# Last feed-forward of a streaming encoder: down-projection by seven products, stream states scaled on ACT

## The chip, the cores and the metric

The kernel runs on one core of a Trainium2 chip. A core has five engines that run side by side, each with its own queue worked off in order: PE (TensorE, matrix products), DVE (VectorE, elementwise), ACT (ScalarE, elementwise and functions), POOL (GpSimd) and SP (SyncE, which here only issues transfers). PE reads its operands from the on-chip memory SBUF and accumulates in PSUM, which has eight banks of 128x512 float32. Transfers between the chip's memory and SBUF are done by 16 DMA engines. The metric is the device time of one execution in microseconds (us).

## The reference, cut to what matters

Two layers of an encoder are applied to 640 tokens of 1024 channels: 512 tokens of a new stream and 16 new tokens for each of eight running streams. Each of the six sub-layers adds its output to its input and normalises. Four of them are feed-forwards; the last sub-layer is one of these. Beside it the kernel finishes the states of the eight running streams of the sub-layer before (a Mamba-2 mixer).

```
x = layer_norm(ALPHA * x + 0.5 * swiglu(x, w_gate, w_up, w_down), g, b)      # four times
def swiglu(x, w_gate, w_up, w_down):
    return (silu(x @ w_gate) * (x @ w_up)) @ w_down          # 1024 -> 2816 -> 1024
h_new = h * exp(cs[:, -1])[..., None, None] + einsum('bsgr,bsgn,bsgrp->bgrpn', to_end, b_c, x_c)
```

Everything is float32.

## The kernel before, in words

**Phases.** `ffn0`, `mix0`, `ffn1`, `ffn2`, `mix1`, `ffn3` run one after the other, all through `ffn()` for the four feed-forwards. The width of 2816 is cut into 22 rows `f` of 128 channels.

**Float32 from three products.** Every operand is split by `split` (lines 94 and 95): ACT rounds it to a high part (a cast), DVE subtracts to get the low part. A product is then three matmuls: high by high, low by high, high by low (`mm3`, line 133).

**Gate and up.** The rows are taken in pairs by `pair`. For each pair, `operands` (lines 320 to 348) loads two blocks of weights and forms the operands of a seven-product (Strassen-Winograd) scheme, and `matrix` (line 358) does seven products of 12 matmuls of 320 columns each (line 355) in three PSUM banks of the pool `a`. Where a bank's running sum is needed twice, `keep` (line 366) copies it to SBUF by ACT into a tile `mx`; PE's next product into that bank waits for the copy. `mx` has three buffers.

**Down-projection.** After each second pair the four rows of the group before are projected by `down`. There are two forms:

- The plain form: for each of five token tiles `t` and two halves `j` of the 1024 channels, `tm_proj` does 12 matmuls of 512 columns in a bank of pool `b`, and DVE adds the bank to the residual `yacc` (line 208).
- `down7`, which the phases listed in `SEVEN` use for four of the six groups: the first four token tiles go by seven products in six banks (`x` and `w` from pool `b`, which has four, `z` from pool `a`), each product on two token tiles `tp` with six matmuls of 512 columns (line 487); the fifth tile goes the plain way (line 507). Sums of rows of the left operand are made earlier by `row_sums` (lines 440 to 445), those of the weights at lines 461 to 464. After each product, `add` takes the bank into `yacc`: for `tp` 1 by DVE (line 495), for `tp` 0 ACT scales it into a tile `ev` (line 498), which a POOL transfer adds to `yacc` (line 499). `ev` has three buffers and is held until the transfer has landed.

Before the change `SEVEN` holds `ffn1` and `ffn2`. The group of two rows at the start and the last group of four, which ends in the layer norm, are plain in every phase.

**Side work of the last phase.** `ssd_states` is a generator that `ffn` steps through at marked points, called ticks: after each gate and each up matrix, and in a plain `down` after token tiles 0, 2 and 4. A step does one of 32 states: a matmul of 48 rows (line 1145), a scaling of the loaded state `h0` by DVE (line 1148), an addition of the matmul's bank by DVE (line 1149), the store (line 1150), and the load of the next state (line 1141). `h0` has two buffers. The first phase has side work of its own (`s5_tables`); `ffn1` and `ffn2` have none.

**Order.** The program is traced as written; a scheduler at build time then orders each engine's queue by readiness in its own model of time and by program order. `tc.issue_after(x)` puts the instructions of the block that run on the engine of `x` behind `x`. A tile's buffer is given out again when all that read it are done.

Of the kernel before, what the change touches and what calls it, by code (L numbers as in the profile page):

```python
# [9 lines left out]
F32 = mybir.dt.float32  # L10
# [3 lines left out]
ALU = mybir.AluOpType  # L14
# [12 lines left out]
HALVES = ((0, 256), (256, 384))  # L27
RAWS = 4
PAIRS = 6
SEVEN = ("ffn1", "ffn2")  # L30
PHASES = ("ffn0", "mix0", "ffn1", "ffn2", "mix1", "ffn3")
LN_OF = {"ffn0": 0, "mix0": 1, "ffn1": 2, "ffn2": 3, "mix1": 4, "ffn3": 5}

# [2 lines left out]
def kernel(ctx: ExitStack, tc: tile.TileContext, I, O, phases=PHASES):  # L36
    nc = tc.nc

    def pool(name, bufs=1, stack=ctx, **kw):
        return stack.enter_context(tc.tile_pool(name=name, bufs=bufs, **kw))  # L40
# [24 lines left out]
    def bank_a():  # L65
        return bank("a")

    def bank_b():
        return bank("b")
# [141 lines left out]
    def ffn(i, ph, last, side=None):  # L211
# [3 lines left out]
        Q = T // 2  # L215
        with ExitStack() as st:
            wk = pool(f"ffn{i}_wk", 1, st, reuse_waits="tile")
            steps = side(wk) if side is not None else iter(())

            def tick(where):  # L220
# [56 lines left out]
            for r in range(2):  # L277
                w = load_w(I["w_gate"][i, 2 + r])
                first[r] = g_row()
                for c in range(2):  # L280
                    p = bank_a()[:, :Q]
# [15 lines left out]

            t2, t3 = (wk.tile([128, 4, Q], F32, name="h", bufs=4) for _ in range(2))
            for k in range(4):
                t1 = wk.tile([128, Q], F32, name="mx", bufs=3)  # L300
                minus(t3[:, k], (1, 1), (0, 1))
                minus(t1, (0, 1), (0, 0))
                for part in (hf32, lf32):
                    V.tensor_tensor(t2[:, k], t3[:, k] if part is hf32 else t2[:, k], quad(part, 0, 0)[:, k], op=ALU.add)
                split(tq[2][:, 0, k], tq[2][:, 1, k], t2[:, k])
                split(tq[1][:, 0, k], tq[1][:, 1, k], t1)
# [52 lines left out]
            def matrix(A, take):  # L359

                x, w, z = (bank_a()[:, :Q] for _ in range(3))
                e = {}

                def keep(n, ps):
                    e[n] = wk.tile([128, Q], F32, name="mx", bufs=3)
                    nc.scalar.copy(e[n], ps)  # L366


                product(x, A, 1, True)
                keep(1, x)  # L370
                product(z, A, 2, True)
                take(0, 0, z, e[1])
                product(x, A, 6, False)
                keep(2, x)
                product(w, A, 5, True)
                keep(5, w)
                product(x, A, 7, False)
                take(1, 1, x, e[5])
                product(w, A, 3, False)
                take(0, 1, w, e[2])  # L380
                product(x, A, 4, False)
                take(1, 0, x, None)

            def pair(f, before=None):
# [26 lines left out]
                for n, take in (("w_gate", gate), ("w_up", up)):  # L411
# [10 lines left out]
                    matrix(A, take)  # L422
                    if n == "w_up" and ph in SEVEN and f < NF - 4:
                        row_sums(f)
# [8 lines left out]
            def row_sums(f):  # L433


                v = [wk.tile([128, 512], F32, name="ev", bufs=3) for _ in range(2)]
                s1, s2, s3, s4 = (v[n // 2][:, n % 2 * 256:n % 2 * 256 + 256].rearrange("p (n c) -> p n c", n=2)
                                  for n in range(4))
                p, q = by_pairs(hf[f]), by_pairs(hf[f + 1])
                V.tensor_tensor(s1, p[:, :, 1], q[:, :, 1], op=ALU.add)  # L440
                V.tensor_tensor(s2, s1, p[:, :, 0], op=ALU.subtract)
                V.tensor_tensor(s3, p[:, :, 0], p[:, :, 1], op=ALU.subtract)
                V.tensor_tensor(s4, q[:, :, 0], s2, op=ALU.subtract)
                o = hs[f] = wk.tile([128, 2, 1024], F32R, name="hs", bufs=2)
                for n in range(2):
                    split(o[:, 0, 512 * n:512 * n + 512], o[:, 1, 512 * n:512 * n + 512], v[n])

            def down7(fs):


                raws, direct = {}, {}
                for f in fs:
                    raws[f] = raw_tile()
                    nc.sync.dma_start(raws[f], I["w_down"][i, f])
                for f in fs:
                    direct[f] = two_units()
                    split2(direct[f], raws[f])

                for f in fs[::2]:
                    (b11, b12), (b21, b22) = ((r[:, :512], r[:, 512:]) for r in (raws[f], raws[f + 1]))  # L460
                    V.tensor_tensor(b22, b22, b12, op=ALU.subtract)
                    V.tensor_tensor(b12, b12, b11, op=ALU.subtract)
                    V.tensor_tensor(b11, b22, b11, op=ALU.add)
                    V.tensor_tensor(b21, b21, b11, op=ALU.subtract)
                T = {}
                for r in range(2):
                    for f in fs[::2]:
                        T[f + r] = two_units()
                        split2(T[f + r], raws[f + r])

                def left(f, p, tp):
                    tok = lambda k, a: ht[f + k][:, :, 256 * tp + 128 * a:256 * tp + 128 * a + 128]
                    if p in (1, 2, 4):
                        return tok(*{1: (0, 0), 2: (1, 0), 4: (1, 1)}[p])
                    o = 256 * {5: 0, 6: 1, 7: 2, 3: 3}[p] + 128 * tp
                    return hs[f][:, :, o:o + 128]

                def right(f, p):
                    return {1: direct[f][:, 0], 2: direct[f + 1][:, 0], 3: direct[f + 1][:, 1],
                            6: T[f][:, 0], 5: T[f][:, 1], 4: T[f + 1][:, 0], 7: T[f + 1][:, 1]}[p]  # L480

                def product(ps, tp, p, first):
                    n = 0
                    for f in fs[::2]:
                        a, b = left(f, p, tp), right(f, p)
                        for u, v in ((0, 0), (1, 0), (0, 1)):
                            nc.tensor.matmul(ps, a[:, u], b[:, v], start=(first and n == 0), stop=(n == 5),
                                             skip_group_check=True)
                            n += 1

                def add(ps, t, j):

                    if t // 2:
                        ya = yacc[:, t, j * 512:j * 512 + 512]
                        V.scalar_tensor_tensor(ya, ps, 0.5 / ALPHA, ya, op0=ALU.mult, op1=ALU.add)
                        return
                    e = wk.tile([128, 512], F32, name="ev", bufs=3)
                    nc.scalar.mul(e, ps, 0.5 / ALPHA)  # L498
                    nc.gpsimd.dma_start(yacc[:, t, 512 * j:512 * j + 512], e, accum_op=ALU.add)  # L499

                t = NT - 1
                for j in range(2):
                    pb = bank_a()
                    mm3(pb, [(ht[f][:, 0, t * 128:t * 128 + 128], ht[f][:, 1, t * 128:t * 128 + 128]) for f in fs],
                        [(direct[f][:, j, 0], direct[f][:, j, 1]) for f in fs])
                    ya = yacc[:, t, j * 512:j * 512 + 512]
                    state["acc"] = V.scalar_tensor_tensor(ya, pb, 0.5 / ALPHA, ya, op0=ALU.mult, op1=ALU.add).ins
                x, w = ([bank_b() for _ in range(2)] for _ in range(2))
                z = [bank_a() for _ in range(2)]
                for p, ps, a, j in ((1, x, 0, 0), (2, z, 0, 0), (5, w, 1, 1), (6, x, 0, 1), (3, w, 0, 1), (7, x, 1, 1),  # L510
                                    (4, x, 1, 0)):
                    for tp in range(2):
                        product(ps[tp], tp, p, p in (1, 2, 5))
                        add(ps[tp], 2 * tp + a, j)

            def down(fs, norm=None):
                if ph in SEVEN and len(fs) == 4 and norm is None:
# [603 lines left out]
    def ssd_states(wk):  # L1121

        el8 = wk.tile([128, 4, 8, 8], F32, name="el8")
        nc.sync.dma_start(el8.rearrange("p g b h -> p g (b h)"), ssd["el"])
        for g, b2, q in ((g, b2, q) for g in range(4) for b2 in range(2) for q in range(2)):
# [11 lines left out]
                        nc.sync.dma_start(xb[rows, 512:640], src(sb, 512, 640))  # L1137
            for h in range(2):
                n = 4 * h + 2 * b2 + q
                h0 = wk.tile([128, 512], F32, name="h0", bufs=2)  # L1140
                nc.sync.dma_start(h0, I["ssd_h0"][g, n])
                yield
                rows = slice(64 * h, 64 * h + 48)
                pst = bank_b()
                nc.tensor.matmul(pst, xb[rows, 512:640].bitcast(F32R), xb[rows, 0:512].bitcast(F32R),  # L1145
                                 start=True, stop=True)
                h4 = h0.rearrange("p (h d) -> p h d", d=64)
                nc.vector.tensor_tensor(h4, h4, el8[:, g, n, :, None].to_broadcast([128, 8, 64]), op=ALU.mult)
                nc.vector.tensor_tensor(h0, h0, pst, op=ALU.add)
                nc.sync.dma_start(O["ssd_s"][g, n], h0)  # L1150

# [514 lines left out]
```

## Time and profile before

| | |
|---|---|
| median of 3 runs | 2604.51 us (2600.36 to 2605.74) |
| the profiled execution | 2604.51 us, its span 2602.8 us |
| last feed-forward's stage, first to last product of its pairs | 2205.1 to 2567 us |
| its states' matmuls | 32, first at 2193.0, last at 2541.8 us |
| groups of `down7` before | four in `ffn1`, four in `ffn2` |

The span runs from the first to the last instruction; 1.7 us of the execution lie outside it. In the rows shown below, a row of the timeline gives the start in us, the length in us from the start of the first to the end of the last instruction, the engine, the line, the tiles written and read, and how many instructions it merges; a bracket at the end tells how long the engine stood idle before it and for whom. The ends of matmuls are modelled, so their pace is read from start to start. A row of the groups gives, behind the bar, the busy us of all and the mean ns of one.

### The profile page before, as it was taken

The numbers are of one execution on the slowest core, as the hardware profiler recorded it, in microseconds if no ns is written. First come the engines' busy times: TensorE is split into PE (matmuls) and PEld (weight loads), VectorE is DVE, ScalarE is ACT, GpSimd is POOL, SyncE is SP. The second block draws the span as 40 slices with busy tenths as digits, with TensorE's granted clock in tenths as the row PEclk, the third lists the DMA queues.
The fourth block names the chain that finished last, engine by engine and source line by source line (L and its number), as shares of the span: only waits on it lengthen the run. The fifth ranks groups of instructions, "written<-read, shape, count | busy, mean of one in ns | idle before, by whom it ended". The sixth has DMA issues, their size and how long they took to land. (4 is left out here: it accounts for less than half of the span.)

```text
span 2602.8 us, 40675 instructions
## 1 busy us (share of the span) xinstructions
PE 2532.5 (97%) x15577; PEld 2294.5 (88%) x15577; DVE 2037.3 (78%) x3726; ACT 1214.9 (47%) x2332; POOL 285.8 (11%) x412
## 2 busy tenths in 40 slices
PE   9999999999969999999999999999999999999998
PEld 8999999887648999998999999889889879998887
DVE  7788777667857988887888887777676799876668
ACT  4443444346533555554455554566565443443332
POOL 0000002110011000003000001311111150000001
PEclk9999999999979999999999999999999999999999
DMA  5332334542211244443144334356564622443442
GB/s 181 106 106 84 112 111 139 168 149 89 82 61 49 76 116 118 118 110 114 49 123 113 102 108 142 112 176 192 162 199 141 236 70 96 157 140 112 133 137 93
DMA packets 173810, 317.43 MB, mean 122 GB/s; under 512 B 19968, under 2 KB 90752, under 8 KB 173104
## 3 DMA queue, kind: packets, MB, share of 16 engines
q1 hardware_dynamic: 163792, 293.83, 35.5%
q0 software_dynamic: 9824, 21.01, 3.9%
q8 instruction: 122, 2.00, 0.3%
q14 instruction: 72, 0.59, 0.1%
HBM read 259.56 MB, written 40.54 MB: 115 GB/s over the span
## 5 line engine op out<-in xcount | busy, mean ns | idle before, releaser
L95 DVE TENSOR_TENSOR w<-raw,w 128x512 fp32r<-128x512 f32 (+1 forms) x617 | 536.9, 893 | 91.9 <-ACT w L94 90.3
L94 ACT CAST w<-raw 128x512 fp32r<-128x512 f32 (+1 forms) x617 | 451.3, 771 | 303.2 <-PE bank L133 113.8
L133 PE MATMUL bank<-xhi,w 128*128 128x256 f32 (+2 forms) x2528 | 557.4, 312 | 14.2 <-ACT xhi L94 6.8
L355 PE MATMUL bank<-xhi,w 128*128 128x320 f32 x2432 | 541.9, 310 | 0.7 <-ACT mx L366 0.4
L133 PEld LDWEIGHTS bank<-xhi,w 128*128 128x128 f32 x2528 | 422.9, 189 | 26.2 <-ACT xhi L94 7.8
L133 PE MATMUL bank<-w,h 128*128 128x512 f32 x1872 | 437.0, 391 | 0.0
L355 PE MATMUL bank<-T,w 128*128 128x320 f32 x2736 | 425.9, 309 | 0.4 <-ACT mx L366 0.4
L133 PEld LDWEIGHTS bank<-w,h 128*128 128x128 f32 x1872 | 348.1, 188 | 75.4 <-issue 3.4
L355 PEld LDWEIGHTS bank<-xhi,w 128*128 128x128 f32 x2432 | 406.0, 188 | 8.3 <-issue 4.4
L355 PEld LDWEIGHTS bank<-T,w 128*128 128x128 f32 x2736 | 406.3, 188 | 1.7 <-ACT mx L366 0.6
L133 PE MATMUL bank<-xlo,w 128*128 128x256 f32 (+2 forms) x1264 | 392.4, 311 | 3.9 <-DVE xlo L95 3.8
L355 PE MATMUL bank<-xlo,w 128*128 128x320 f32 x1216 | 375.0, 308 | 0.0
L133 PEld LDWEIGHTS bank<-xlo,w 128*128 128x128 f32 x1264 | 238.9, 189 | 6.5 <-DVE xlo L95 5.1
L355 PEld LDWEIGHTS bank<-xlo,w 128*128 128x128 f32 x1216 | 228.0, 188 | 0.3
L208 DVE SCALAR_TENSOR_TENSOR yacc<-bank,yacc 128x512 f32<-128x512 f32 x160 | 109.5, 687 | 81.1 <-PE bank L133 80.2
L366 ACT COPY mx<-bank 128x320 f32<-128x320 f32 x228 | 96.5, 424 | 133.3 <-PE bank L355 132.6
L95 DVE TENSOR_TENSOR w<-sw,w 128x1024 fp32r<-128x1024 f32 x76 | 93.0, 1223 | 51.4 <-ACT w L94 51.2
L94 ACT CAST w<-sw 128x1024 fp32r<-128x1024 f32 x76 | 79.8, 1050 | 100.0 <-DVE sw L334 99.0
L499 POOL DMA_DIRECT2D yacc<-ev x56 | 48.6, 902 | 652.1 <-ACT ev L498 597.9
L133 PE MATMUL bank<-w,og 128*128 128x512 f32 x432 | 106.3, 400 | 2.8 <-DVE og L1460 2.8
L133 PEld LDWEIGHTS bank<-w,og 128*128 128x128 f32 x432 | 80.6, 191 | 21.1 <-DVE og L1460 4.6
L394 ACT ACTIVATE s<-s 128x320 f32<-128x320 f32 x108 | 50.8, 471 | 88.4 <-DVE s L392 88.2
(416 smaller groups left out, 3306.4 us busy)
## 6 DMA issues: line engine op xcount, KB each, us to landing
raw<-in_w_gate_dram SPq DMA_DIRECT2D x88, 512.0 KB, 3.8
raw<-in_w_up_dram SPq DMA_DIRECT2D x88, 512.0 KB, 4.0
raw<-in_w_down_dram SPq DMA_DIRECT2D x88, 512.0 KB, 3.6
raw<-in_m_in_dram SPq DMA_DIRECT2D x52, 512.0 KB, 4.6
yacc<-ev POOLq DMA_DIRECT2D x56, 256.0 KB, 4.2
raw<-in_m_out_dram SPq DMA_DIRECT2D x24, 512.0 KB, 3.8
csb<-cs_d SPq DMA_DIRECT2D x20, 512.0 KB, 5.1
h<-in_ssd_h_dram SPq DMA_DIRECT2D x16, 512.0 KB, 6.1
```

The lines of the kernel that those rows point to most:

```text
L94: nc.scalar.copy(hi, src)
L95: return nc.vector.tensor_tensor(lo, src, hi.bitcast(F32), op=ALU.subtract)
L133: state["pe"] = nc.tensor.matmul(ps, a, b, start=(k == 0), stop=(k == n - 1)).ins
L208: state["acc"] = nc.vector.scalar_tensor_tensor(ya, pb, scale, ya, op0=ALU.mult, op1=ALU.add).ins
L355: nc.tensor.matmul(ps, A[p][:, a, k * 128:k * 128 + 128], B[p][b][:, k, :], start=(first and n == 0), stop=(n == 11), skip_group_check=True)
L366: nc.scalar.copy(e[n], ps)
L394: state["silu"] = nc.scalar.activation(t, ps, AF.Silu).ins
L499: nc.gpsimd.dma_start(yacc[:, t, 512 * j:512 * j + 512], e, accum_op=ALU.add)
```

## The change

1. `ffn3` joins `SEVEN`: four of its six groups go through `row_sums` and `down7`. `down7` gets three ticks of its own, at its start and after the products numbered 5 and 3.
2. The scaling of a state goes from one DVE instruction of 128x512 to eight ACT instructions of 128x64, one for each head, with a scale for each partition.
3. In the phases that have side work (`ffn0` and `ffn3`), `mx` and `ev` have two buffers in place of three.
4. `h0` of the states has one buffer in place of two, and the room on chip for the descriptors of POOL's transfers is halved.

```
-SEVEN = ("ffn1", "ffn2")
+SEVEN = ("ffn1", "ffn2", "ffn3")
...
+            few = side is not None
...
-                    e[n] = wk.tile([128, Q], F32, name="mx", bufs=3)
+                    e[n] = wk.tile([128, Q], F32, name="mx", bufs=2 if few else 3)
...
-                v = [wk.tile([128, 512], F32, name="ev", bufs=3) for _ in range(2)]
+                v = [wk.tile([128, 512], F32, name="ev", bufs=2 if few else 3) for _ in range(2)]
...
-                    e = wk.tile([128, 512], F32, name="ev", bufs=3)
+                    e = wk.tile([128, 512], F32, name="ev", bufs=2 if few else 3)
...
                 t = NT - 1
+                tick(0)
                 for j in range(2):
...
                         add(ps[tp], 2 * tp + a, j)
+                    if p in (5, 3):
+                        tick(2 if p == 5 else 4)
...
-                h0 = wk.tile([128, 512], F32, name="h0", bufs=2)
+                h0 = wk.tile([128, 512], F32, name="h0", bufs=1)
...
-                h4 = h0.rearrange("p (h d) -> p h d", d=64)
-                nc.vector.tensor_tensor(h4, h4, el8[:, g, n, :, None].to_broadcast([128, 8, 64]), op=ALU.mult)
+                for k in range(8):
+                    nc.scalar.mul(h0[:, 64 * k:64 * k + 64], h0[:, 64 * k:64 * k + 64], el8[:, g, n, k:k + 1])
...
-    nc = _bacc.Bacc("TRN2", target_bir_lowering=False, num_devices=1, dynamic_dma_scratch_size=4096)
+    nc = _bacc.Bacc("TRN2", target_bir_lowering=False, num_devices=1, dynamic_dma_scratch_size=2048)
```

More of the change, by code (lines that the diff above doesn't have):

```diff
@@ L299, in ffn @@
             for k in range(4):
-                t1 = wk.tile([128, Q], F32, name="mx", bufs=3)
+                t1 = wk.tile([128, Q], F32, name="mx", bufs=2 if few else 3)
                 minus(t3[:, k], (1, 1), (0, 1))
```

## The prediction

> **What bounds the kernel now.** I read the page's head first, then the waits of the last feed-forward's stage, then the chain that ended last inside it, then two stretches side by side: one of `ffn1`, where `down7` already runs, and one of `ffn3`.
>
> ```profile
> span 2602.8 us, 40675 instructions
> PE 2532.5 (97%) x15577; PEld 2294.5 (88%) x15577; DVE 2037.3 (78%) x3726; ACT 1214.9 (47%) x2332; POOL 285.8 (11%) x412
> ...
> 2218.61 12.51 PE bank L355 x84
> 2231.11 0.43 PE bank L1145
> ...
> 850.00:1180.00 330.00, 329.84 (x2000) 310.94 (x2000) 278.34 (x407) 174.48 (x267) 24.39 (x29) 1.00 0.41 111
> 2206.00:2541.00 335.00, 335.00 (x1928) 302.31 (x1928) 244.61 (x361) 123.92 (x200) 0.00 (x0) 1.00 0.42 135
> ```
>
> The third and fourth rows are from the chain of waits between 2200 and 2260 us, which is made of PE alone: a matrix (84 matmuls, 12.51 us), a state's matmul (0.43), the next matrix. The last two rows are the stretches; the columns behind the length are PE, PEld, DVE, ACT, POOL busy, granted clock, DMA share, GB/s. PE has no gap in the second stretch, the clock is full, DVE is at 244.61/335 = 73%, ACT at 37%. A modelled busy time alone proves little; the pace does:
>
> ```profile
> 976.45 5.63 PE L133 MATMUL bank<-w,h 128*128 128x512 f32 x24
> 987.36 11.04 PE L487 MATMUL bank<-w,hs 128*128 128x512 f32 x48
> 998.24 1.52 PE L487 MATMUL bank<-w,h 128*128 128x512 f32 x6
> 1050.47 5.63 PE L133 MATMUL bank<-w,h 128*128 128x512 f32 x24
> ...
> 2257.34 5.78 PE L133 MATMUL bank<-w,h 128*128 128x512 f32 x24
> 2263.48 11.18 PE L133 MATMUL bank<-w,h 128*128 128x512 f32 x48
> 2274.59 0.50 PE L1145 MATMUL bank<-xb 48*128 48x512 f32 x1
> 2338.24 5.76 PE L133 MATMUL bank<-w,h 128*128 128x512 f32 x24
> ```
>
> From start to start, 48 matmuls of `down7` take 998.24 - 987.36 = 10.88 us, 0.2267 each. In `ffn3`, 48 of the plain form take 2274.59 - 2263.48 = 11.11, the little more being the state matmuls at both ends. A group (two pairs and a down) takes 1050.47 - 976.45 = 74.02 us in `ffn1` and 2338.24 - 2257.34 = 80.90 in `ffn3`. So PE's instruction stream is the time of this stage: fewer matmuls shorten it, and work on other engines is free until PE waits for it.
>
> **Part 1, the seven products.** A plain group is 5 token tiles x 2 halves x 12 = 120 matmuls of 512 columns. `down7` is 24 for the fifth tile and 7 x 2 x 6 = 84, so 108. Four groups save 4 x 12 = 48 matmuls x 0.2267 = **10.9 us**, and nothing else is on PE's stream. The two groups' periods agree: 80.90 - 2.72 (12 x 0.2267) - 74.02 leaves 4.16 for seven states, 0.59 each, near the 0.43 of a state's row plus refilling beside it. A group of the new `ffn3` should take 80.90 - 2.72 = 78.2 us.
>
> What it adds stands in these groups of instructions, of the whole trace:
>
> ```profile
> L208 DVE SCALAR_TENSOR_TENSOR yacc<-bank,yacc 128x512 f32<-128x512 f32 x160 | 109.5, 687 | 81.1 <-PE bank L133 80.2
> L495 DVE SCALAR_TENSOR_TENSOR yacc<-bank,yacc 128x512 f32<-128x512 f32 x56 | 38.5, 688 | 44.3 <-PE bank L487 44.3
> L498 ACT ACTIVATE ev<-bank 128x512 f32<-128x512 f32 x56 | 33.4, 597 | 76.5 <-PE bank L487 76.2
> L95 DVE TENSOR_TENSOR w<-raw,w 128x512 fp32r<-128x512 f32 x400 | 276.7, 719 | 51.1 <-ACT w L94 50.5
> L95 DVE TENSOR_TENSOR w<-raw,w 128x1024 fp32r<-128x1024 f32 x216 | 261.1, 1219 | 40.7 <-ACT w L94 39.8
> L94 ACT CAST w<-raw 128x512 fp32r<-128x512 f32 x400 | 232.2, 622 | 96.0 <-PE bank L355 32.0 <-issue 17.0 <-PE bank L133 15.0
> L94 ACT CAST w<-raw 128x1024 fp32r<-128x1024 f32 x216 | 220.3, 1049 | 207.2 <-PE bank L133 98.8 <-DVE raw L334 72.2 <-DVE yacc L208 18.1
> L461 DVE TENSOR_TENSOR raw<-raw 128x512 f32<-128x512 f32 x16 | 10.3, 682 | 0.0
> L440 DVE TENSOR_TENSOR ev<-hf 128x256 f32<-128x256 f32 x16 | 6.7, 416 | 0.0
> L94 ACT CAST hs<-ev 128x512 fp32r<-128x512 f32 x32 | 19.5, 615 | 17.3 <-DVE ev L441 17.3
> L95 DVE TENSOR_TENSOR hs<-ev,hs 128x512 fp32r<-128x512 f32 x32 | 21.8, 686 | 0.0
> L1148 DVE TENSOR_TENSOR h<-h,el 128x512 f32<-128x512 f32 x32 | 21.8, 685 | 3.8 <-DMA h<-in_ssd_h_dram 3.6
> ```
>
> DVE, one group. Removed: 10 additions (0.687) and 8 splits (0.719), 12.6 us. Added: 8 wide splits (1.219) 9.8, eight sums of weights (0.682) 5.5, 9 additions (0.688) 6.2, eight sums of rows (0.416) 3.3, four splits of them (0.686) 2.7, 27.5 us. So +14.9 a group, +60 in all; part 2 takes 32 x 0.685 = 22 back. DVE in the stretch of `ffn3` becomes about (244.6 + 38)/324 = 87%, against 278.34/330 = 84% in `ffn1`, where PE stood still for 0.16 us of 330. ACT, one group: removed 8 x 0.622 = 5.0; added 8 x 1.049, 7 x 0.597, 4 x 0.615 = 15.0; +10.0 a group, +40 in all. The loads are the same four blocks a group. I cost all of it at nothing: PE's stream covers it in `ffn1` with the same operations. Without that cover the 60 us of DVE would be the price.
>
> **Part 2, scaling by ACT.** The nearest row is eight ACT instructions of the same size with a scale for each partition, in the mixer:
>
> ```profile
> 1717.38 1.76 ACT L1363 ACTIVATE xe<-bank,tok 128x64 f32<-128x64 f32 x8
> ...
> 2296.40 0.48 DVE L400 TENSOR_TENSOR hf<-bank,mx 128x320 f32<-128x320 f32 x1
> 2298.34 0.48 DVE L400 TENSOR_TENSOR hf<-bank,mx 128x320 f32<-128x320 f32 x1
> 2301.58 0.43 ACT L366 COPY mx<-bank 128x320 f32<-128x320 f32 x1
> ```
>
> Eight cost 1.76 us where DVE took 0.685; 32 states are 56 us of ACT, which goes to about (124 + 40 + 55)/324 = 68%. ACT works in order, so the copy to `mx` that PE waits for (line 366) can stand behind such a block: PE has one product of 12 matmuls, 12.51/7 = 1.79 us, less the copy's 0.43, so 1.36 us of grace. A block of 1.76 that starts just as the copy falls due costs PE 0.4 us; if that befell all 32 states, 13 us. From below, the 0.685 gone from DVE gains nothing, DVE not being the bound. I take zero, the row of the ACT load in `ffn1` (174.48/330, 53%, no stall) being nearest. The block also brings a wait to ACT, for the landing of `h0`; behind it stand casts of weights and the same copies, so a load that lands later than the scheduler's model has it stalls PE as well.
>
> The Trainium skill speaks against this part. "ScalarE: Activation LUTs", section "Rules for kernel authors", sends multiplications to VectorE and not to ScalarE; its section "What ACT_TABLE_LOAD costs" gives 186 ns + 0.833 ns a column + 93 ns for a scale that is read from memory, less 93 where instructions follow on, which as an estimate is 8 x 0.24 = 1.9 us a state. The trace agrees on the duration (1.76); by the rule ACT would pay more than DVE is spared, and the whole would come out as the second rival below.
>
> **Part 3, two buffers for `mx` and `ev`.** For `mx`: the third copy's buffer was last needed by the addition at 2298.34, and the next matrix's first copy runs at 2301.58, 2.8 us after that addition's end. PE's order is the same in every matrix of both phases, with two products (3.6 us) between the two, so nothing; an addition that DVE brings over 2.8 us late would hold ACT and then PE. `ev` is tighter, and `ffn1` shows it with three:
>
> ```profile
> DMA to landing us min/median/max: 3.3/4.2/6.0
> ...
> 984.37 0.86 POOL L499 DMA_DIRECT2D yacc<-ev  x1 [56.78 <-ACT ev L498]
> 988.96 1.76 POOL L499 DMA_DIRECT2D yacc<-ev  x2 [3.73 <-DMA yacc<-ev]
> ...
> 991.68 0.60 ACT L498 ACTIVATE ev<-bank 128x512 f32<-128x512 f32 x1 [2.12 <-PE bank L487]
> 997.14 0.59 ACT L498 ACTIVATE ev<-bank 128x512 f32<-128x512 f32 x1
> ```
>
> The second transfer adds to the same piece of `yacc` as the first, so it waits for its landing: 988.96 + 4.2 = 993.2 before its buffer is free. With two buffers the fourth copy, at 991.68 before, waits for that, 1.5 us. Followed on, the sixth (997.14) waits for the fourth's landing at about 998.2, ends at 998.8, and the last product's first half, which began at 998.24, comes 0.6 us late. It needs that bank; its other half does not and can go first. With landings of 6.0 throughout it would be some 5 us a group. From below zero. I take 0.2 a group, 0.8 us: nearest to the other half going first.
>
> **Part 4, one `h0`, half the descriptor room.** The next load now waits for the store's landing.
>
> ```profile
> 2326.39 0.34 SPq L1150 DMA_DIRECT2D out_ssd_s_dram<-h  x1
> 2329.40 0.33 SPq L1141 DMA_DIRECT2D h<-in_ssd_h_dram  x1
> ...
> out_ssd_s_dram<-h SPq DMA_DIRECT2D x32, 256.0 KB, 2.1
> h<-in_ssd_h_dram SPq DMA_DIRECT2D x30, 256.0 KB, 2.8
> ...
> L1149 DVE TENSOR_TENSOR h<-h,bank x32: 674/678/689, 2195.3 to 2543.7; 128x512 f32<-128x512 f32 x32
> ```
>
> Between matrices the load already leaves 3.0 us after the store, longer than the 2.1 a store takes, so nothing is lost there. The chain of one state is load 2.8, scaling 1.76, addition 0.68, store 2.1: 7.3 us, with some 3 us of queues about 10.5. The states now come every (2543.7 - 2195.3)/31 = 11.2 us. It fits, closely. It touches PE only through banks: `x` and `w` of `down7` take all four of pool `b`, so a state stepped on after product 5 gets one only when product 3 has been added (12 to 24 matmuls, 2.7 to 5.4 us later), and a state that still holds one delays `w`; other products can run meanwhile, so I cost it at nothing. Behind the waiting load on SP stand the weights' loads, which are issued a matrix ahead. Half the descriptor room: no row shows POOL waiting for room; it waits for the copy or the landing. Nothing, up to a landing (4.2) a transfer.
>
> **Sum.** 2604.51 - 10.9 + 0.8 = **2594.4 us**. The profiled execution is the median itself; its span is 2602.8, with 1.7 outside that I keep.
>
> **The rivals.**
> - *Copies wait for `ev`, and PE for the copies* (or the halved room holds POOL back). For it: the chain of landings above; against it: the other half of each product. 0.6 to 3 us a group, say 1.5 over the 0.2 taken: 2594.4 + 5 = 2599.6. Chance 0.19.
> - *Scaling blocks ACT*: 0.4 us for each of 32 states, and splits late for the next matrix: 2594.4 + 13 = 2607. For it: ACT's order; against it: 53% without a stall in `ffn1`, single instructions of 0.22 us between which a copy can be put. Chance 0.12.
> - *The states become the end* (slower). The one `h0` makes one chain of 31 links from 2195.3. At c us a link the last addition is at 2195.3 + 31 c, with its store (2.1) and the program's end some 5 us more. It decides over the forecast from c = 12.6, is slower than before from 13.0, and at 13.5 gives 2621, the 1.7 included. Against it: 10.5 worked out, and links get shorter once the pairs are done. Chance 0.06.
>
> **How the numbers follow.** The forecast has 0.63. A measurement of this kernel tells about 0.2%, 5.2 us, from no change: faster is below 2599.3, slower above 2609.7. Faster: 0.63, half of the first rival, and 0.04 of the second, 0.76. Slower: 0.06 and 0.02 of the second, 0.08. Same: 0.16. The range goes from 2590 (no stall, and the runs' scatter of 2600.36 to 2605.74 below it) to 2605, which leaves out the slower case and the upper part of the second rival.
>
> **What would show it.** Right: groups of `ffn3` 78.2 us apart; 12 `down7` groups and 84 transfers at line 499; the final down's first matmul some 10 us earlier than now; still no PE among the waits of the stage; the last addition of a state before 2560. Wrong: PE idle in line 487 for the copies at 498 (first rival), PE or line 366 behind the scaling (second), or states after the final layer norm (third); a group of 80 us or more means that the saved matmuls became waits.

## The result and the profile after

| | before | after |
|---|---|---|
| median | 2604.65 us (2600.36 to 2605.74) | 2618.99 us (2616.33 to 2623.68) |
| ratio, 95% interval | | 1.006 (1.0041 to 1.0079) |
| profiled execution, span | 2604.51, 2602.8 us | 2620.05, 2618.4 us |

The change made the kernel 14 us slower, where 10 us less had been forecast. Lines of the new kernel stand one further than before up to `down7` (the copy to `ev` is L499, its transfer L500, a product L488), and the state's matmul is L1149. The page's head, then the stretch of the last feed-forward that the prediction showed:

```profile
span 2618.4 us, 41048 instructions
PE 2532.5 (97%) x15529; PEld 2291.1 (88%) x15529; DVE 2071.7 (79%) x3770; ACT 1312.2 (50%) x2632; POOL 310.0 (12%) x440
...
2206.00:2541.00 335.00, 319.28 (x1782) 285.08 (x1781) 267.07 (x390) 207.67 (x459) 23.10 (x27) 0.96 0.52 150
```

The 48 matmuls are gone (15577 - 15529), yet PE, which had no gap in these 335 us, now stands still for 15.7 of them, and its granted clock is 0.96. I measure the stage from the first matmul of the first plain down to the first of the final one. The rows of PE's timeline at both ends, before and then after:

```profile
2190.18 2.92 PE L133 MATMUL bank<-w,h 128*128 128x512 f32 x12
...
2566.91 27.58 PE L133 MATMUL bank<-w,h 128*128 128x512 f32 x120
```

```profile
2189.03 2.92 PE L133 MATMUL bank<-w,h 128*128 128x512 f32 x12
...
2582.41 13.79 PE L133 MATMUL bank<-w,h 128*128 128x512 f32 x59
```

376.7 us became 393.4, where 376.7 - 10.9 = 365.8 had been worked out. The rest of the span, up to that point and behind it, moved by 1.2 us at most. So 27.6 us were lost inside the stage. PE's waits there, and then one group in time, by the timelines of PE, ACT and POOL:

```profile
PE bank L1149 <- ACT ev L499: 14.6, 4, 4.4
PE bank L356 <- ACT mx L367: 1.1, 3, 0.5
```

```profile
2266.65 0.83 ACT L1152 ACTIVATE h<-h,el 128x64 f32<-128x64 f32 x3 [1.24 <-DVE raw L464]
2267.39 2.94 ACT L94 CAST w<-raw 128x1024 fp32r<-128x1024 f32 x3
2270.23 1.29 ACT L1152 ACTIVATE h<-h,el 128x64 f32<-128x64 f32 x5
2271.43 1.05 ACT L499 ACTIVATE ev<-bank 128x512 f32<-128x512 f32 x2
...
2272.31 1.75 POOL L500 DMA_DIRECT2D yacc<-ev  x2 [5.60 <-ACT ev L499]
...
2278.55 0.60 ACT L499 ACTIVATE ev<-bank 128x512 f32<-128x512 f32 x1 [3.64 <-DMA yacc<-ev]
2280.18 0.60 ACT L499 ACTIVATE ev<-bank 128x512 f32<-128x512 f32 x1 [1.03 <-DMA yacc<-ev]
...
2269.77 6.79 PE L488 MATMUL bank<-w,hs 128*128 128x512 f32 x29
2280.83 0.50 PE L1149 MATMUL bank<-xb 48*128 48x512 f32 x1 [4.27 <-ACT ev L499]
2281.26 3.90 PE L488 MATMUL bank<-w,hs 128*128 128x512 f32 x9
2285.09 0.49 PE L1149 MATMUL bank<-xb 48*128 48x512 f32 x1
```

Read it from the bottom. PE stops 4.27 us in front of a state's matmul, which needs a bank that ACT has yet to copy out. That is the copy at 2280.18. ACT stands 1.03 us before it and 3.64 us before the copy ahead of it, because both `ev` buffers are held by transfers still landing. Those left together at 2272.31, since ACT made two copies back to back at 2271.43, behind scalings of a state and three casts of weights. The products behind the state's matmul in PE's queue had to wait with it. A stop of PE like this happens once in each of the four groups. The back-to-back copies do not: in the second and the fourth group the copies are 3.3 to 3.7 us apart, and the two transfers leave together because the first of them waits for a landing before it, of 6.6 and 6.9 us.

The time lost is larger than the stops. The nine matmuls behind this one took 2285.09 - 2281.26 = 3.83 us, 0.43 each and not 0.2267. The windows, where the third number from the end is the granted clock, say why:

```profile
2270.00:2276.00 6.00, 6.00 (x28) 4.93 (x27) 5.85 (x8) 4.15 (x10) 1.75 (x2) 1.00 0.88 266
2276.00:2281.00 5.00, 0.73 (x4) 0.31 (x2) 1.66 (x3) 1.42 (x3) 0.85 (x1) 1.00 0.79 211
2281.00:2286.00 5.00, 5.00 (x13) 3.43 (x14) 2.42 (x3) 3.22 (x10) 0.89 (x2) 0.66 0.56 97
...
2358.00:2364.00 6.00, 3.32 (x14) 2.29 (x12) 2.85 (x5) 2.68 (x6) 1.81 (x3) 0.93 0.86 180
2364.00:2370.00 6.00, 6.00 (x15) 4.53 (x15) 3.68 (x5) 2.98 (x8) 1.72 (x2) 0.50 0.69 152
```

After each of these stops the clock is halved for some 4 to 6 us. The rows of PE behind the other three stops:

```profile
2363.50 0.79 PE L1149 MATMUL bank<-xb 48*128 48x512 f32 x1 [2.68 <-ACT ev L499]
2364.22 6.14 PE L488 MATMUL bank<-w,hs 128*128 128x512 f32 x14
2370.34 1.52 PE L488 MATMUL bank<-w,h 128*128 128x512 f32 x6
...
2450.75 4.21 PE L488 MATMUL bank<-w,hs 128*128 128x512 f32 x9
2454.89 0.69 PE L1149 MATMUL bank<-xb 48*128 48x512 f32 x1
...
2535.64 5.79 PE L488 MATMUL bank<-w,hs 128*128 128x512 f32 x14
2541.41 1.55 PE L488 MATMUL bank<-w,h 128*128 128x512 f32 x6
```

Start to start, 9 + 14 + 9 + 14 = 46 matmuls took 3.83 + 6.12 + 4.14 + 5.77 = 19.86 us in place of 46 x 0.2267 = 10.43, so 9.4 us more. With the waits (15.7) that makes 25.1 of the 27.6 us. The Trainium skill, "TensorE: Matmul & The Clock Gate", section "Why this matters for your kernels", asks for no idle gap of TensorE over about 3 us, since one idle window takes the clock to half. The trace agrees on the half clock, and shows it after an idle time of 2.68 us too.

### The profile page after: what moved, and what is told of

Same layout as the page of the kernel before. It is cut to its first block, busy times and chain, and to the rows that moved or that the text cites. A ratio compares the mean times of both kernels' runs of the same rounds, so it can differ in the third digit from the quotient of the medians.

```text
span 2618.4 us, 41048 instructions
## 1 busy us (share of the span) xinstructions
PE 2532.5 (97%) x15529; PEld 2291.1 (88%) x15529; DVE 2071.7 (79%) x3770; ACT 1312.2 (50%) x2632; POOL 310.0 (12%) x440
## 5 line engine op out<-in xcount | busy, mean ns | idle before, releaser
L95 DVE TENSOR_TENSOR w<-raw,w 128x512 fp32r<-128x512 f32 (+1 forms) x617 | 553.5, 920 | 95.0 <-ACT w L94 94.1
L94 ACT CAST w<-raw 128x512 fp32r<-128x512 f32 (+1 forms) x617 | 466.0, 794 | 221.1 <-DVE raw L335 75.4
L133 PE MATMUL bank<-xhi,w 128*128 128x256 f32 (+2 forms) x2528 | 555.9, 312 | 14.3 <-ACT xhi L94 7.2
L356 PE MATMUL bank<-xhi,w 128*128 128x320 f32 x2432 | 544.1, 310 | 2.5 <-ACT mx L367 2.2
L356 PE MATMUL bank<-T,w 128*128 128x320 f32 x2736 | 427.0, 309 | 0.7 <-DVE s L393 0.5
L356 PEld LDWEIGHTS bank<-xhi,w 128*128 128x128 f32 x2432 | 406.4, 188 | 11.9 <-ACT mx L367 5.1
L356 PEld LDWEIGHTS bank<-T,w 128*128 128x128 f32 x2736 | 406.3, 188 | 3.3 <-ACT mx L367 1.2
L356 PE MATMUL bank<-xlo,w 128*128 128x320 f32 x1216 | 375.0, 308 | 0.0
L133 PE MATMUL bank<-w,h 128*128 128x512 f32 x1488 | 348.6, 391 | 0.0
L133 PEld LDWEIGHTS bank<-w,h 128*128 128x128 f32 x1488 | 276.5, 188 | 58.8 <-issue 1.2
L356 PEld LDWEIGHTS bank<-xlo,w 128*128 128x128 f32 x1216 | 228.1, 188 | 0.4
L500 POOL DMA_DIRECT2D yacc<-ev x84 | 73.0, 897 | 1019.9 <-ACT ev L499 828.6
L488 PE MATMUL bank<-w,hs 128*128 128x512 f32 x576 | 142.8, 408 | 0.0
L488 PEld LDWEIGHTS bank<-w,hs 128*128 128x128 f32 x576 | 113.6, 198 | 26.4 <-issue 2.1
L496 DVE SCALAR_TENSOR_TENSOR yacc<-bank,yacc 128x512 f32<-128x512 f32 x84 | 57.3, 687 | 67.0 <-PE bank L488 67.0
L208 DVE SCALAR_TENSOR_TENSOR yacc<-bank,yacc 128x512 f32<-128x512 f32 x120 | 81.9, 686 | 35.1 <-PE bank L133 34.6
```

What stands on the lines that cost most here:

```text
L94: nc.scalar.copy(hi, src)
L95: return nc.vector.tensor_tensor(lo, src, hi.bitcast(F32), op=ALU.subtract)
L133: state["pe"] = nc.tensor.matmul(ps, a, b, start=(k == 0), stop=(k == n - 1)).ins
L208: state["acc"] = nc.vector.scalar_tensor_tensor(ya, pb, scale, ya, op0=ALU.mult, op1=ALU.add).ins
L356: nc.tensor.matmul(ps, A[p][:, a, k * 128:k * 128 + 128], B[p][b][:, k, :], start=(first and n == 0), stop=(n == 11), skip_group_check=True)
```

## The experiments

The theory is the one just read: copies that come late and two `ev` buffers held by landings, in front of an engine whose order is fixed. Its rivals are the scaling on ACT, the place and the bank of the states' matmuls, the one `h0`, and simply too much work on DVE and ACT. All runs start from the kernel after, and line numbers shift by up to five with the edits. Stages are those of one profile each, and a profiled execution lies up to 4.3 us from its run's median (bank_a), so a difference of a few us between two stages is not sure by itself. Ratios are against the kernel before.

| run | median us | ratio, 95% interval | stage us | PE's costliest wait there: us in sum, times |
|---|---|---|---|---|
| no_seven | 2604.67 | 0.9997 to 1.0016 | 376.8 | none |
| dve_scale | 2623.24 | 1.0061 to 1.0102 | 394.3 | copy to ev 16.7, 4 |
| nostates_ev3 | 2577.90 | 0.9889 to 0.9918 | 346.9 | none |
| nostates_ev2 | 2583.22 | 0.9909 to 0.9939 | 353.5 | copy to ev 4.2, 4 |
| scr512 | 2632.96 | 1.0093 to 1.0123 | 403.3 | copy to ev 23.9, 4 |
| ev3_scr512 | 2610.99 | 1.0016 to 1.0035 | 380.9 | copy to ev 8.3, 4 |
| shared3 | 2608.48 | 1.001 to 1.0029 | 379.4 | copy to ev 5.9, 4 |
| late_ticks | 2615.36 | 1.0028 to 1.0057 | 388.9 | copy to ev 12.4, 7 |
| bank_a | 2612.21 | 1.0016 to 1.0039 | 386.3 | copy to mx 7.3, 7 |
| shared3_late | 2604.86 | 0.9991 to 1.0012 | 380.1 | copy to ev 7.5, 3 |
| pairs_only | 2618.08 | 1.0044 to 1.0072 | 390.7 | DVE's addition 10.9, 4 |
| pairs_shared3 | 2606.88 | 1.0007 to 1.0025 | 381.3 | copy to ev 8.4, 3 |
| dve_add | 2606.80 | 1.0005 to 1.0024 | 378.2 | DVE's addition 3.5, 2 |
| dve_add_late | 2601.99 | 0.9992 to 1.0013 | 374.7 | DVE's addition 3.1, 2 |
| shared3_dve_scale | 2605.93 | 1.0008 to 1.0027 | 380.5 | DVE's addition 4.9, 2 |
| dve_add_late_h2 | 2601.13 | 0.9978 to 1.0 | 372.5 | DVE's addition 2.6, 2 |
| dve_add_pairs_h2 | 2603.82 | 0.9993 to 1.0013 | 372.3 | a cast 2.1, 4 |
| pairs_shared3_h2 | 2603.70 | 0.9989 to 1.0007 | 372.9 | copy to ev 2.5, 4 |

### Which part costs: the products or the scaling

**no_seven** leaves everything but the seven products.

```
-SEVEN = ("ffn1", "ffn2", "ffn3")
+SEVEN = ("ffn1", "ffn2")
```

> The last feed-forward's down-projection in the plain form again; all other parts of the change stay (scaling by ACT, two mx and ev buffers, one h0, half the descriptor room). Theory A: 2602 to 2607 us, as before the change. Theory B: the scaling blocks ACT in the matrices too, 2608 to 2618 us.

**dve_scale** gives the scaling of the states back to DVE.

```
-                for k in range(8):
-                    nc.scalar.mul(h0[:, 64 * k:64 * k + 64], h0[:, 64 * k:64 * k + 64], el8[:, g, n, k:k + 1])
+                h4 = h0.rearrange("p (h d) -> p h d", d=64)
+                nc.vector.tensor_tensor(h4, h4, el8[:, g, n, :, None].to_broadcast([128, 8, 64]), op=ALU.mult)
```

> The changed kernel with the states scaled by DVE again, as before; seven products, two ev buffers and one h0 stay. Theory A: the landings still hold two buffers, so waits of 1 to 4 us in each of the four groups remain, 2608 to 2620 us. Theory B: the copies come on time, 2594 to 2602 us. If both act together, between: 2602 to 2610 us.

The stretch 2206 to 2541 of no_seven, and PE's waits of dve_scale:

```profile
2206.00:2541.00 335.00, 335.00 (x1924) 301.90 (x1923) 228.71 (x333) 179.35 (x435) 0.00 (x0) 1.00 0.43 137
```

```profile
PE bank L1149 <- ACT ev L499: 16.7, 4, 5.0
```

With the scaling on ACT, two buffers of `mx`, one `h0` and the halved room, but plain products, PE has no gap and the time is that of before. These parts cost nothing by themselves. And without the scaling, ACT has a quarter less work (153.48 us of the stretch in place of 207.67) and PE stands still as long. The theory that the scaling holds up the copies falls, though one block of it stands in the queue in the group shown.

### What the seven products give without the states

Both runs leave the states out. **nostates_ev3** has three buffers of `ev` and `mx`, since `few` is then false; **nostates_ev2** has two of `ev`.

```
-    if "mix1" in phases and "ffn3" in phases:
-        sides["ffn3"] = ssd_states
...
-                    e = wk.tile([128, 512], F32, name="ev", bufs=2 if few else 3)
+                    e = wk.tile([128, 512], F32, name="ev", bufs=2 if ph == "ffn3" else 3)
```

> The states of the running streams are left out (that output isn't written); the last feed-forward is then like the two in the middle, with seven products and three buffers of mx and ev. The ceiling: 2604.3 less 32 states at 0.59 us less 10.9 us of matmuls, 2574 us (2571 to 2578) by all theories; if it is over 2580, seven products in this phase cost something that the middle ones do not show.

> As the run without states, with two ev buffers in the last feed-forward. Theory A: PE waits for ev copies in line 488 although there is no state, 2 to 5 us a group with the slow matmuls, 2582 to 2595 us. Theory F (two buffers hurt only beside the states' ACT work and transfers): within 3 us of the run with three, 2571 to 2579 us.

PE's timeline of nostates_ev3 at three groups' starts, PE's waits of nostates_ev2, and how long the transfers of `ev` took to land from 2250 to 2560 us, first in nostates_ev2 and then in the changed kernel:

```profile
2333.57 5.63 PE L133 MATMUL bank<-w,h 128*128 128x512 f32 x24
2407.60 5.63 PE L133 MATMUL bank<-w,h 128*128 128x512 f32 x24
2481.63 5.63 PE L133 MATMUL bank<-w,h 128*128 128x512 f32 x24
```

```profile
PE bank L488 <- ACT ev L499: 4.2, 4, 1.1
PE bank L488 <- DVE yacc L496: 0.5, 3, 0.2
```

```profile
DMA to landing us min/median/max: 3.2/4.1/5.2
```

```profile
DMA to landing us min/median/max: 3.2/4.1/8.0
```

A group takes 74.03 us, as in `ffn1`. The stage of 346.9 is 376.7 - 10.9 for the matmuls and 18.9 for 32 states, 0.59 each, the figure that the prediction drew from the groups' periods. So the saving is real and complete where nothing else runs. Two buffers of `ev` cost 353.5 - 346.9 = 6.6 us, 1.65 a group, even without the states (5.3 by the medians). Two transfers leave together there as well, and ACT stands 4.1 us for their landing, but PE only 1.1. Beside the states the middle landing is as long and the longest are not: nine of the 28 take longer than any in nostates_ev2. What makes them longer was not tried.

### The buffers of `ev`

A third `ev` takes 2 KB more of each partition. **ev3_scr512** takes the space from the descriptor room, and **scr512** shrinks that room alone.

```
-                    e = wk.tile([128, 512], F32, name="ev", bufs=2 if few else 3)
+                    e = wk.tile([128, 512], F32, name="ev", bufs=3)
...
-    nc = _bacc.Bacc("TRN2", target_bir_lowering=False, num_devices=1, dynamic_dma_scratch_size=2048)
+    nc = _bacc.Bacc("TRN2", target_bir_lowering=False, num_devices=1, dynamic_dma_scratch_size=512)
```

> The changed kernel with three buffers of ev again in the last feed-forward; the room for them comes from the descriptor room, 512 in place of 2048. Theory A (a state's matmul in the middle of down7 waits for a bank, which waits for an ev copy by ACT, which waits for a transfer's landing to free one of two buffers): the four waits of 2.8 to 4.5 us in front of the states' matmuls shrink below 1 us each and the half-clock matmuls behind them go, 2594 to 2600 us. Theory B (ACT is late because it scales the states): no change, 2615 to 2622 us. Theory C (the bank alone: any state in the middle of down7 waits, whatever ev has): 2608 to 2620 us.

> The changed kernel with the descriptor room at 512 in place of 2048 and nothing else: the control for the run with three ev buffers. All theories but one expect 2616 to 2624 us, as the changed kernel. Theory D (the smaller room holds POOL's transfers back): over 2625 us, with POOL waiting longer between the transfers of line 500.

**shared3** keeps the room and lets `mx` and `ev` of `ffn3` take turns in one set of three buffers of 128x512.

```
-                    e[n] = wk.tile([128, Q], F32, name="mx", bufs=2 if few else 3)
+                    e[n] = (wk.tile([128, 512], F32, name="ev", bufs=3)[:, :Q] if ph == "ffn3" else
+                            wk.tile([128, Q], F32, name="mx", bufs=3))
```

> The changed kernel, but in the last feed-forward the copies mx and ev come from one set of three buffers of 128x512 (in place of two of each; the matrices use them in their time, down7 in its own), with the descriptor room at 2048; the first feed-forward has its three mx again. Theory A (two ev buffers wait for landings): PE's waits on ev copies fall from 14.6 us to under 4, no half-clock matmuls, 2595 to 2603 us. Theory F (the copies are late because ACT and the transfers carry the states beside down7, whatever the buffers): over 2608 us, PE still waiting in front of the states' matmuls.

POOL's waits of scr512, then PE's waits of shared3:

```profile
POOL yacc L500 <- issue: 82.5, 24, 6.3
```

```profile
PE bank L1151 <- ACT ev L501: 5.9, 4, 2.2
PE bank L490 <- ACT ev L501: 2.7, 4, 1.1
PE bank L357 <- ACT ev L369: 1.3, 4, 0.4
```

The third buffer takes 403.3 - 380.9 = 22.4 us off the stage at a room of 512, and 393.4 - 379.4 = 14.0 at 2048: half of the loss. The medians give 22.0 and 10.5. In shared3 `mx` has a third buffer too, but PE's waits for `mx` had been 1.1 us in all. The halved room of 2048 is no cost that the runs show, a room of 512 is: there POOL waits 82.5 us for something that the profile does not show, and with the change's 2048 the same row had 0.8 us.

### Where the states are stepped on

**late_ticks** moves the two inner ticks of `down7` behind its last product, **bank_a** gives the state's matmul a bank of the other pool, and **shared3_late** is shared3 with the edit of late_ticks.

```
-                    if p in (5, 3):
-                        tick(2 if p == 5 else 4)
+                for n in (2, 4):
+                    tick(n)
```

```
-                pst = bank_b()
+                pst = bank_a()
```

> The changed kernel with the two steps of the states that stand inside down7 (after products 5 and 3) moved behind its last product. Theories A and C (a state's matmul inside down7 stops PE): the four waits and the slow matmuls go, 2593 to 2600 us, and line 488 runs at 0.227 us a matmul throughout. Theory B: ACT does the same work, 2610 to 2620 us.

> The changed kernel with the state's bank taken from pool a (of which down7 gives back four in its course) in place of pool b (all four in use by x and w). Theories A and C: the state's matmul no longer waits for an ev copy, 2594 to 2602 us. Theory B: 2612 to 2622 us. If PE's stop only moves to the product that needs the late copy itself, a wait of about 1 us in line 488 in each group and about 2600 us.

> As the run with three shared buffers, and the two steps of the states inside down7 moved behind its last product. Theory A: the same as that run within 3 us. Theory C (a state's matmul inside down7 makes PE stop where the products could have gone on): 3 to 8 us faster than that run, 2592 to 2599 us.

**pairs_only** has no tick in `down7` and steps twice after each up matrix; **pairs_shared3** is that with shared3.

```
-                tick(0)
...
-                    if p in (5, 3):
-                        tick(2 if p == 5 else 4)
...
                     tick("gate" if n == "w_gate" else "up")
+                    if n == "w_up":
+                        tick("up")
```

> The changed kernel with no step of the states inside down7: its three ticks are dropped and each up matrix is followed by two steps. Two buffers of mx and ev stay. The stage of the last feed-forward (first plain down to last) took 376.7 us before and 393.4 changed. Theory A+F (two buffers cost some 7 us by themselves, as without states; the rest is the states' scaling and transfers in the middle of down7): 372 to 376 us for the stage, 2599 to 2604 us. Theory A alone (the buffers' cost is the whole with states, too): over 382 us, 2608 us or more.

> The same with the three shared buffers for mx and ev in the last feed-forward. Theory A+F: nothing is left that stops PE, the stage at 366 to 370 us, 2593 to 2598 us, faster than both kernels. Theory G (seven products and the states are together too much for DVE or ACT wherever they stand): over 375 us, 2603 us or more.

None of these brings the stage under 380 us. With the state's matmul out of the way PE stops at the next product whose bank is not copied (L488, or L356 in the next matrix). In the stage PE stands still for 16.3 us in late_ticks and 14.3 in bank_a, against 15.7, but in shorter pieces, and the granted clock of the stage is 0.99 in both, against 0.97. These two get 4.5 and 7.1 us of the stage back; beside three buffers the same move gives nothing (380.1 against 379.4). So the state's matmul was mainly the place of the stop and not its cause. In pairs_only, where no state is stepped in `down7`, PE stood 10.9 us for DVE's additions there.

### Without copies and transfers

**dve_add** lets DVE make all 14 additions of `down7` in `ffn3`; **dve_add_late** adds the edit of late_ticks.

```
-                    if t // 2:
+                    if t // 2 or few:
```

> The changed kernel with all fourteen additions of down7 in the last feed-forward done by DVE, as its lower seven were: no copy by ACT, no transfer at line 500 and no ev buffer in them. Theory A (the copies to ev are late, because two buffers wait for landings, and whatever PE does next stops behind them): no wait of PE on ev, no half-clock matmuls, 2593 to 2600 us. Theory B (ACT is late because it scales the states): 2605 to 2618 us. Theory E (DVE, with 19 us more, becomes the bound): PE waits on DVE at line 496, 2600 to 2612 us.

> As the run with all additions by DVE, and the two steps of the states inside down7 moved behind its last product. Theory A: the copies were the whole cause, so within 3 us of the run with all additions by DVE. Theory C (a state inside down7 costs by itself, through the banks): 4 to 10 us faster than that run, 2591 to 2597 us.

PE's waits of dve_add and its stretch 2206 to 2541:

```profile
PE bank L488 <- DVE yacc L496: 3.5, 2, 1.9
PE bank L356 <- ACT mx L367: 1.9, 4, 1.2
PE bank L356 <- ACT w L94: 1.6, 3, 0.7
...
2206.00:2541.00 335.00, 327.47 (x1875) 291.85 (x1874) 293.06 (x432) 199.53 (x446) 0.00 (x0) 1.00 0.42 136
```

The stops of over 2 us are gone and the clock is full, at the price of DVE being busy for 293.06/335 = 87%. dve_add is a little slower than the kernel before (1.0005 to 1.0024), dve_add_late as fast (0.9992 to 1.0013). So the copies and their transfers are what made the long stops.

### What is left: ACT, or the one `h0`

**shared3_dve_scale** is shared3 with the edit of dve_scale. **dve_add_late_h2** is dve_add_late with a second `h0`, **dve_add_pairs_h2** is dve_add with the ticks of pairs_only and a second `h0` (both with a room of 512, which `ffn3` then has no use for), and **pairs_shared3_h2** is pairs_shared3 with a second `h0` and a room of 1024.

```
-                h0 = wk.tile([128, 512], F32, name="h0", bufs=1)
+                h0 = wk.tile([128, 512], F32, name="h0", bufs=2)
```

> Three shared buffers, the states' steps inside down7 as in the changed kernel, but scaled by DVE. The stage was 379.4 us with scaling by ACT. If the scaling by ACT in front of the copies is what the buffers leave over: 366 to 372 us, 2594 to 2599 us. If it is the states' transfers or banks inside down7: 376 us or more, 2603 us or more, with PE still waiting for copies.

> All additions of down7 in the last feed-forward by DVE, ticks at the end of down7, and two buffers of h0 again (the descriptor room is 512, which this phase no longer needs). One buffer of h0 as the remaining cost: the stage falls from the 374.7 us that it had with one h0 towards the ideal 365.8, below 370, and the kernel is at 2594 to 2598 us, ratio about 0.997. VectorE's load as the remaining cost (293 of 335 us, in fixed order): the stage stays at 373 to 377 us and the kernel at 2600 to 2604.

> As before it, but no state inside down7: two after each up matrix, with two buffers of h0. If states inside down7 are what holds its products up, the stage is at 366 to 369 us and the kernel at 2594 to 2598; if VectorE's own work of down7 is too late whatever the states do, 373 us or more and 2600 or more. Two states at one point can also stop TensorE in front of the second state's matmul: then waits for h appear in front of line 1149.

> The copies and transfers of down7 stay, three buffers are shared by mx and ev, two states follow each up matrix, and h0 has its second buffer again (descriptor room 1024). If the chain of the one h0 pushed the scalings into down7 in the run without the second buffer (stage 381.3 us), the stage falls to 366 to 370 us and the kernel to 2594 to 2598, ratio about 0.997, faster than both. If the work of down7 on VectorE and ScalarE is late by itself, the stage stays at 375 us or more and the kernel at 2602 or more. A descriptor room of 1024 that is too small would show as idle time of POOL with the cause issue, which 2048 did not have.

The stretch of dve_add_pairs_h2, PE's waits in the stage of pairs_shared3_h2, and two rows of ACT and PE behind that stage's end:

```profile
2206.00:2541.00 335.00, 330.59 (x1916) 298.61 (x1915) 298.69 (x440) 197.10 (x428) 0.00 (x0) 1.00 0.40 129
```

```profile
PE bank L492 <- ACT ev L503: 2.5, 4, 0.8
PE bank L357 <- DVE w L95: 1.6, 3, 0.5
```

```profile
2563.13 0.83 ACT L1153 ACTIVATE h<-h,el 128x64 f32<-128x64 f32 x3 [6.72 <-DMA h<-in_ssd_h_dram]
...
2564.63 28.39 PE L133 MATMUL bank<-w,h 128*128 128x512 f32 x114 [1.56 <-ACT h L94]
```

Whether ACT or DVE scales the states matters as little with three buffers as with two (380.5 against 379.4). The second `h0` takes the stage from 381.3 to 372.9 where the transfers stay and no state is stepped in `down7`, though the descriptor room differs between those two runs; POOL's waits of the second one show only 0.7 us with the cause issue. But 3.6 us of these 8.4 come back behind the stage: in the last rows shown ACT stands 6.72 us for an `h0` to land, the casts of the final down's operand stand behind it, and PE stops there. From the final down's first matmul to the end it takes 2601.3 - 2561.4 = 39.9 us, against 36.3 in pairs_shared3 and 35.9 before. By the ratios (1.0016 and 0.9998) the second `h0` is worth 4.7 us. Without the transfers it is 2.2 us of the stage (374.7 to 372.5), which is not clear of the scatter.

So all three last versions have a stage of 372 to 373 us, 7 above the 365.8, and pairs_shared3_h2 loses 4 more behind it. The waits of PE that the profile shows make 3.6 to 4.2 of the 7, the longest 1.3. The medians lie within 0.2% of before, and dve_add_late_h2 alone reaches an interval that ends at 1.0; no version tried is clearly faster than the kernel before.

## Why the prediction was wrong

- **Part 1, the saving** of 10.9 us was right: 48 matmuls less, and nostates_ev3 shows all of it. "I cost all of it at nothing: PE's stream covers it in `ffn1`" holds there, at 281.70/335 = 84% of DVE. Beside the states it does not quite: the best three versions keep 7 us over the ideal stage.
- **Part 2, the scaling**, at nothing, was right: no_seven and dve_scale. A state's eight instructions took 2.03 us (65.0/32) and not 1.76. The Trainium skill, "ScalarE: Activation LUTs", section "What ACT_TABLE_LOAD costs", led to an estimate of 1.9 us; the trace agrees within 7%. The rival made of it, 13 us by ACT's order, was not what stopped PE in the stage. The warning beside it, that ACT waits for an `h0` to land with casts behind, came true in pairs_shared3_h2, at the final down.
- **Part 3 is the step that failed**, by its price for `ev` (`mx`, taken at nothing, made PE wait 1.1 us). "I take 0.2 a group, 0.8 us: nearest to the other half going first." Measured are 6.6/4 = 1.65 us a group without the states and 14.0/4 = 3.5 with them (1.3 and 2.6 by the medians). The chain of landings in the prediction was the right mechanism, and its first rival, the same mechanism at a higher price, is near the figure without states; its 1.5 a group "over the 0.2 taken" would be 6.0 us, though, and the sum there adds 5.2. Three things were missing. The other half did not go first: PE's queue has a fixed order, and whatever was put behind the waiting matmul waited too. The chain was reckoned from copies made on time, as `ffn1` has them; beside the states some came late. And it was reckoned with landings of 4.2 us, where some took up to 8.0; "with landings of 6.0 throughout it would be some 5 us a group" is the prediction's own figure for that. How the loss beside the states divides between the last two stays open.
- **Part 4** failed at "other products can run meanwhile, so I cost it at nothing": PE stopped in front of the state's matmul itself. bank_a and late_ticks show that another place for it mainly moves the stop. That the states do not become the end was right: 32 additions from 2194.2 to 2561.2 us are (2561.2 - 2194.2)/31 = 11.8 us a link, under the 12.6 from which that rival decided. But one `h0` had its price elsewhere, 4.7 us by the ratios of pairs_shared3 and pairs_shared3_h2.
- **Not in the prediction at all**: the half clock behind a stop, 9.4 us, about as much as the whole saving.

```profile
L1153 DVE TENSOR_TENSOR h<-h,bank x32: 675/679/689, 2194.2 to 2561.2; 128x512 f32<-128x512 f32 x32
...
L1152 ACT ACTIVATE h<-h,el 128x64 f32<-128x64 f32 x256 | 65.0, 336 | 15.7 <-DMA h<-in_ssd_h_dram 14.3 <-DVE raw L464 1.2
```

In sum: 27.6 us were lost against the ideal stage. 14.0 go with the third buffer (10.5 by the medians). With the states out of `down7` and the second `h0` the stage falls by 6.5 more (379.4 to 372.9), but 4.0 of these return at the final down; the ratios, 1.002 and 0.9998, put the two together at 5.7. How that divides stays open: the ticks alone gave nothing (381.3 against 379.4), and a second `h0` without them was not tried beside the transfers. The last 7 were not taken apart either: whether DVE's share (298.69/335 = 89% in the stretch of dve_add_pairs_h2), the order of its and ACT's queues, or the pace of the loads makes them stays open.

## What to carry to other kernels

A buffer that is held until a transfer lands belongs to a chain: count its links with copies that come late, not as a neighbouring stage has them on time. An engine with a fixed order does not step round a late operand, so "something else can run meanwhile" must be read from the queue's order, item by item. Where PE has no gap, each short stop counts in full and may cost as much again in clock (a stop of 2.68 us was followed by 14 matmuls that took 6.12 us in place of 3.17): work on other engines is not free merely because their shares stay below 90%.

## What the runs showed of the hardware

- The clock can be halved after stops of under 3 us, and the length of a stop alone does not decide it. In bank_a a stop of 1.75 us was followed by twelve matmuls in 2288.01 - 2283.55 = 4.46 us, 0.37 each, and the granted clock from 2285 to 2287 us was 0.50. In late_ticks one of 2.57 us was followed by twelve in 3.04 us, the modelled end of the last one included, 0.25 each, at a clock of 1.00. What else decides it, no run shows.

```profile
2283.55 4.62 PE L488 MATMUL bank<-w,hs 128*128 128x512 f32 x12 [1.75 <-ACT ev L499]
2288.01 0.45 PE L356 MATMUL bank<-xhi,w 128*128 128x320 f32 x2
...
2444.64 3.04 PE L488 MATMUL bank<-w,hs 128*128 128x512 f32 x12 [2.57 <-ACT ev L499]
2449.13 3.04 PE L488 MATMUL bank<-w,h 128*128 128x512 f32 x12 [1.45 <-ACT ev L499]
```

- A descriptor room of 512 in place of 2048 made the kernel 2632.96 - 2618.99 = 14.0 us slower (12.5 by the ratios, 1.0108 and 1.006).
